# A third Strassen–Winograd level inside two of seven inner products, for three pairs of instances

## The chip, the cores and the metric

The kernel runs on one core of one Trainium2 chip. The metric is the device time of one execution in microseconds (us). Three runs of the kernel before the change are given, and one more execution of it was profiled.

## The reference

```python
batch, seq, hidden, n_experts, expert_hidden = 16, 512, 512, 8, 2048
probs = softmax(router_logits)                       # over the 8 experts
for e in range(n_experts):
    output += probs[:, :, e:e+1] * np.matmul(x, expert_weights[e])
```

The eight weighted products are one matrix product. Its left side has 16 x 512 = 8192 rows, one for each token, and 8 x 512 = 4096 columns: the token's x, scaled by the probability of each expert. Its right side is the stack of the experts' weights, 4096 rows and 2048 columns. The output is 8192 x 2048 in float32.

## The kernel before

**Two levels of a seven-product scheme.** The kernel multiplies in the Strassen–Winograd manner: a 2 x 2 x 2 product of blocks is made of seven block products instead of eight, and of sums and differences of blocks before and after. The outer level splits the output columns in two, the experts in two (0 to 3, 4 to 7) and the rows into 256-row blocks taken in twos, `a = 2q` and `b = 2q + 1`, for q from 0 to 15. Its seven products are called by the number r, and there are 16 instances (r, q) of each: `product(r, q)`. The instances with r = 1 ("P1") multiply the rows of block `a`, experts 0 to 3, by `right[1]`, the weights of these experts for the first half of the columns. They store float32 results in DRAM buffers called `kept`.

An instance has 256 rows, an inner dimension of 4 x 512 = 2048 and 1024 columns. It is split once more the same way: rows in two halves of 128 (`HP`), the inner dimension in two halves of eight chunks of 128 (`K8 = 8`; `t[0]` and `t[1]` on the left), columns in two halves of 512 (`NB`). So there are seven inner products, in the order `STEPS = (1, 5, 6, 2, 7, 3, 4)`. Each is one *step*: eight matmuls, 128 x 128 by 128 x 512, that accumulate into one bank of PSUM (`Product.step`, `mm`). `Left.op` and `Right.op` give the operands of a step. Inner products 1 and 5 both take the first half of the inner dimension, `t[0]`: product 1 its first 128 rows with the right block `w[1]`, product 5 its last 128 rows with `w[5]`, the difference of two right blocks.

**Banks.** A product uses three banks, `x`, `q` and `b`. `x` takes steps 1, 6, 7 and 4 one upon another, `q` steps 5 and 3, `b` a copy of `x` after step 1 and then step 2. After each step `Product.post` has ScalarE (ACT) copy a bank, or VectorE (DVE) add a bank and a tile in SBUF. All banks come from one pool of eight.

**Stages and slots.** Two instances run as a pair through one *stage* of 14 *slots*: step 1 of the first, step 1 of the second, step 5 of the first, and so on. Instances (1, 0) and (1, 1) are computed at the start in plain form. Stage 0 is the pair (1, 2) and (1, 3), stages 1 to 3 are (1, 4) and (1, 5), (1, 6) and (1, 7), (1, 8) and (1, 9). Stage 4 pairs (2, 9) with (1, 10).

**Order.** From stage 0 on, every engine's instructions keep the order in which the program records them. For DVE that order comes from a small planner: `later(cost, make)` queues a piece of DVE work, `slack()` moves a model clock by one slot (1.73) and runs queued pieces as long as DVE's model clock lies more than `LAG` behind PE's, and `need(task)` runs the queue up to a piece that the next step reads. `queue_lefts` queues the left blocks of the next stage (`make` for `t[0]` and `t[1]`, `queue_s2` and `queue_i` for the sums among them). `start_loads` and `finish_loads` fetch the next x and probability blocks two stages ahead; x is transposed by DMA on SP's queue. `hooks` are actions at a (stage, slot), for example the weight sums `sums_at`. Outputs are stored by POOL's DMA queue.

The left blocks `z`, the inner sums `d`, the half outputs `h` and the weights `w` live in pools of 8, 3, 12 and 15 tiles.

Of the kernel before, what the change touches and what calls it, by code (L numbers as in the profile page):

```python
# [31 lines left out]
def kernel(  # L32
# [7 lines left out]
    nc = tc.nc  # L40
    P = 128
# [8 lines left out]
    C = H // P  # L50
# [23 lines left out]
    def h_tile(shape, dtype):  # L74
        return hpool.tile(shape, dtype, name="h", tag="h")
# [8 lines left out]
    with tc.tile_pool(name="psum0", bufs=1, space=bass.MemoryType.PSUM) as psum0:  # L84
# [2 lines left out]
        every = psum0.tile([P, 8, NB], f32, name="every")  # L87
        for i in range(WARM):
            nc.tensor.matmul(every[:, i % 8, :], zero[:, 0:P], zero, start=True, stop=True)
    psum = ctx.enter_context(tc.tile_pool(name="psum", bufs=8, space=bass.MemoryType.PSUM))  # L90

    last = {}
    ordered = [False]
# [12 lines left out]
    def tt(o, a, b, op):  # L106
        dve(nc.vector.tensor_tensor(out=o, in0=a, in1=b, op=op))  # L107
# [14 lines left out]

    def bank():
        return psum.tile([P, NB], f32, name="ps", tag="ps")

    def mm(ps, z, w, start, stop):
        note(nc.tensor.matmul(ps, z, w, start=start, stop=stop, skip_group_check=True))  # L127
# [3 lines left out]
    def new_w():  # L131
        return wpool.tile([P, K8, NB], f16, name="w", tag="w")
# [31 lines left out]
    def inner_sums(b, t7=None):  # L164

        w = {1: b[0, 0], 2: b[1, 0], 3: b[1, 1], 7: t7 or b[0, 1]}

        def step(p, x, y):
            if p not in w:
                w[p] = new_w()  # L170
            tt(w[p], x, y, SUB)
        return w, {5: lambda: step(5, b[0, 1], b[0, 0]), 6: lambda: step(6, b[1, 1], w[5]),
                   4: lambda: step(4, b[1, 0], w[6]), 7: lambda: step(7, b[1, 1], b[0, 1])}

    def softmax(lg, J, pf):
        mx = h_tile([P, J], f32)
# [85 lines left out]

    def early_xp1(j, d):
        t, rows = j // 2 - 2, ds(j % 2 * P, P)
        ps = bank()
        for c in range(C):
            mm(ps[:, ds(c * P, P)], xs0[:, j, ds(c * P, P)], ident, c == 0, c == C - 1)
        evacuate(xp1[t][0][:, :, rows], ps.rearrange("p (c t) -> p c t", c=C), 0)
        ps = bank()
        mm(ps, ones, d.rearrange("p e t -> p (e t)"), True, True)  # L270
        evacuate(xp1[t][1][:, :, rows], ps.rearrange("p (e t) -> p e t", e=HE), 1)

# [33 lines left out]
    load_logits()  # L306
    early_z0(1, ds_[1])
    for n in range(2):
        ps = [bank() for _ in range(4)]
        for e in range(HE):  # L310
            if n == 0 and e < 2:
                early_z0(e + 2, ds_[e + 2])
                if e == 0:
                    ds_.append(diag_e(3))
            if n == 0 and e == 2:
                ph0.append(early_p(1))
                ds_ = [diag_j(j) for j in range(4, 8)]
                softmax_of_all()
                w, sums = inner_sums(b11, new_w())
            for c in range(C):  # L320
                for j in range(4):
                    mm(ps[j], z0[j][:, e, c], b11[e // 2, n][:, e % 2 * C + c, :],
                       e + c == 0, e == HE - 1 and c == C - 1)
            if n == 1:
                for j in ((4, 5), (6, 7), (), ())[e]:
                    early_xp1(j, ds_[j - 4])
                if e == 1:
                    sums[5]()
        for j in range(4):
            o = half()  # L330
            act(nc.scalar.copy(o, ps[j]))
            sp(kept[j // 2][n].rearrange("(p j) m -> j p m", j=2)[j % 2], o)
# [9 lines left out]
    class Task:  # L342


        def __init__(self, cost, make):
            self.cost, self.make, self.done = cost, make, False
# [17 lines left out]
        (queue.appendleft if first else queue.append)(t)  # L364
        return t

    def slack():
        clock["dve"] = max(clock["dve"], clock["pe"])
        clock["pe"] += SLOT
        while queue and clock["dve"] < clock["pe"] - LAG:  # L370
            queue.popleft().run()

    def evacuated():
        clock["dve"] = max(clock["dve"], clock["pe"]) + 0.69


    x_dram = {}
# [48 lines left out]
    class Left:  # L426
# [36 lines left out]
        def op(self, p):  # L463
# [4 lines left out]
                    3: (self.i, 0), 7: (self.i, 1)}[p]  # L468
            return t[:, :, ds(i * HP, HP)]

    class Right:


# [16 lines left out]
    class Product:  # L490
# [7 lines left out]
        def step(self, p):  # L498
            b = "q" if p in (5, 3) else "b" if p == 2 else "x"
            if p in (1, 5):  # L500
                self.banks[b] = bank()
            z, w = self.left.op(p), self.right.op(p)
            for k in range(K8):
                mm(self.banks[b], z[:, k, :], w[:, k, :], p in (1, 5) and k == 0, k == K8 - 1)
# [27 lines left out]
        def post_on_base(self, p, x, q, b):  # L532
# [13 lines left out]
            else:  # L546
                tt(o[tn], q if p in (5, 3) else x, base, ADD)


    def out_rows(q, odd, cols, tn):  # L550
        t, n = tn
# [63 lines left out]
    def product(r, q, **how):  # L615
        left, loads = left_of(r, q)
        lefts[r, q] = left
        p = None
        if r == 1:
            def sink(tn, o):  # L620
                pool(kept_rows(q)(tn), o)
            p = Product(right[1], left, sink)
        elif r == 2:
            if q >= 9:
                base = products[1, q].o.__getitem__
            else:
                base = bases[2, q] = Base(kept_rows(q))
            p = Product(right[2], left, to_out(q, 0, 0), base)
        elif r == 5:
            bases[6, q] = m1 = Base(kept_rows(q))  # L630
            m1.task = {}

            p = Product(right[5], left, to_out(q, 1, 0))
        elif r == 6:
            m1 = bases[6, q]

            def base(tn):
                need(m1.task[tn])
                return m1.t[tn]
            p = Product(right[6], left, to_out(q, 0, 1), base)  # L640
        elif r == 7:
            base = bases[7, q] = Base(lambda tn: out_rows(q, 0, 1, tn))
            p = Product(right[7], left, to_out(q, 1, 1), base)
        elif r == 4:
            p = Product(right[4], left, to_out(q, 1, 0, accum_op=ADD), products[7, q].o.__getitem__)
        else:
            p = Product(right[3], left, to_out(q, 0, 1, accum_op=ADD), **how)
        p.loads = loads
        products[r, q] = p
        return p  # L650
# [23 lines left out]
    def queue_left(left):  # L674
        if not left.task:
            left.queue_make(0)
            left.queue_s2()
            left.queue_make(1)

    def queue_lefts(stage):  # L680
        if stage < len(stages):
            for p in stages[stage]:
                queue_left(p.left)

    def run(stage):
        some = stages[stage]
        for p in some:
            p.left.queue_i()
        n = 0
        for i in range(len(some[0].steps)):  # L690
            for p in some:
                for make in hooks.get((stage, n), ()):
                    make()
                p.step(p.steps[i])
                slack()
                p.post(p.steps[i])
                n += 1
                if n == 1:
                    queue_lefts(stage + 1)
                if n == late.get(stage, 1):  # L700
                    start_loads(stage + 2)
                if n == 5:
                    store_loads(stage + 1)
                if n == 7:
                    finish_loads(stage + 2)
# [3 lines left out]
            at(stage, slot, lambda tn=tn: base.fetch(tn))  # L709


    for q in (2, 4, 6, 8):
        add(product(1, q), product(1, q + 1))
    for q in range(9, 15):
        add(product(2, q), product(1, q + 1))
    forget(*range(0, 18, 2))
    rest = [15] + list(range(9))
    for i in range(0, 10, 2):
        k = add(product(2, rest[i]), product(2, rest[i + 1]))
        for slot, tn in zip((8, 10, 12, 13), INNER):  # L720
            for q in rest[i:i + 2]:
                if q < 9:
                    fetch_at(k if tn == (1, 0) else k - 1, 3 if tn == (1, 0) else slot, bases[2, q], tn)
    xs.clear()
    k5 = add(product(5, 0), product(5, 1))
# [64 lines left out]
    def wedge_at(stage, slot, kn, e, then):  # L790
        made = []

        def begin():
            casts, made_ = wedge(kn, e)
            casts()
            made.extend(made_)

        def go_on():
            for make in made:
                later(1.22, make)  # L800
        at(stage, slot, begin)
        at(*then, go_on)
# [9 lines left out]
    def sums_at(stage, slot, r, of, ps):  # L812
        def go():
            if right[r].w is None:
                right[r].sums = right[r].build(of)
            for p in ps:
                right[r].queue_sum(right[r].sums, p)
        at(stage, slot, go)
    sums_at(3, 3, 2, b21, (5,))
    sums_at(3, 5, 2, b21, (6,))  # L820
    sums_at(3, 7, 2, b21, (7,))
    sums_at(3, 12, 2, b21, (4,))
    for i, (kn, e) in enumerate((kn, e) for kn in ((0, 0), (1, 0), (1, 1)) for e in range(2)):
        wedge_at(4 + i, 2, kn, e, (4 + i, 11))

    def fetch_at_w(stage, slot, of, what, kn):
        at(stage, slot, lambda: of.__setitem__(kn, fetch_w(what, kn)))
# [174 lines left out]
            post(p)  # L1002
    finish.step, finish.post = step_at_end, post_at_end

    need_first = [right[1].task[p] for p in (6, 7, 4)]
    for p in (2, 3):
        lefts[1, p].queue_make(0)
# [39 lines left out]
```

## Time and profile before

| | |
|---|---|
| median of 3 runs | 1376.0 us (1375.86 to 1377.01) |
| profiled execution | 1376.63 us, span 1374.9 us |
| instructions | 17480, of them 6390 matmuls and as many weight loads |
| DMA | 338.02 MB, mean 246 GB/s |

The profile is of one execution. PE is TensorE's matmuls, PEld its weight loads, which overlap them; SP and the names with a q are queues of DMA issues. In the lists of groups a row gives the line, engine and operation, output<-input with shapes and count, then busy time and the mean length of one in ns, then the idle time of the engine just before and what ended it. In the timeline a row gives start and length in us, engine, line, operation and count, and in brackets the idle time before it and its releaser. A matmul's row lasts until its result is out, longer than the time after which the next one starts. Helpers record most operations, so nearly all matmuls have line 127 and nearly all two-input DVE operations line 107.

### The profile page before, as it was taken

Reading aid. Unit: us, or ns where it says so; the run is one execution under the profiler, and the core shown is the slowest. Engines: PE = TensorE matmul, PEld = TensorE weight load, DVE = VectorE, ACT = ScalarE, POOL = GpSimd, SP = SyncE. Lnnn points to the kernel's source line nnn. Section 1 sums busy time; section 2 is a strip of 40 time slices with the busy share of each in tenths; the row PEclk is TensorE's granted clock in tenths of the full one; section 3 lists DMA queues with packets and bytes.
Section 4 is the critical chain, followed back from the end, with each engine's and each line's share of the span. In section 5 each row is a group of like instructions: output and inputs, shape, how many; then the busy total and the mean of one; then the engine's idle time right before and its main releaser. Section 6 shows DMA issues by size and latency. Waiting matters only on the chain.

```text
span 1374.9 us, 17480 instructions
## 1 busy us (share of the span) xinstructions
PE 1367.3 (99%) x6390; PEld 622.0 (45%) x6390; DVE 1108.6 (81%) x1290; ACT 183.1 (13%) x317; POOL 411.8 (30%) x652
## 2 busy tenths in 40 slices
PE   8999999999999999999999999999999999999998
PEld 4444444444444444444444444444444444444444
DVE  5846757669889888798897988889889898988882
ACT  3222111100011111111111100000000000222221
POOL 3222333241223342334232122242333322232221
PEclk9999999999999999999999999999999999999999
DMA  9998999999898998899898998988898979987786
GB/s 183 222 261 205 211 248 265 241 299 378 240 323 249 285 300 246 259 261 265 245 276 263 338 392 219 224 236 212 229 237 223 247 204 316 249 187 177 166 150 106
DMA packets 191271, 338.02 MB, mean 246 GB/s; under 512 B 52944, under 2 KB 86992, under 8 KB 187472
## 3 DMA queue, kind: packets, MB, share of 16 engines
q0 software_dynamic: 88688, 185.12, 55.8%
q1 hardware_dynamic: 98464, 123.34, 30.8%
q10 hardware_dynamic: 4032, 28.44, 5.3%
q8 instruction: 50, 0.82, 0.2%
q14 instruction: 37, 0.30, 0.1%
HBM read 207.65 MB, written 156.43 MB: 265 GB/s over the span
## 4 chain that ended last, share of the span: by engine, by line
PE 98%; DMA 2%; POOL 0%; issue 0%; ACT 0%; POOLq 0%
PE ps L127 98%; DMA w<-wd 1%; DMA w<-in_expert_weights_dram 1%; POOL w L121 0%; ACT h L999 0%; POOL ident L211 0%; POOLq L211 0%; POOLq L1031 0%
## 5 line engine op out<-in xcount | busy, mean ns | idle before, releaser
L127 PE MATMUL ps<-w,z 128*128 128x512 f16 x5416 | 1177.3, 379 | 1.3 <-DMA w<-in_expert_weights_dram 1.1
L127 PEld LDWEIGHTS <-z 128*128 128x128 f16 x5416 | 529.7, 98 | 638.6 <-DMA w<-in_expert_weights_dram 1.3
L121 POOL DMA_DIRECT2D out_dram<-h x380 | 248.9, 672 | 746.4 <-ACT h L540 373.7
L107 DVE TENSOR_TENSOR h<-ps,h 128x512 f32<-128x512 f32 x415 | 282.5, 687 | 207.6 <-PE ps L127 192.8
L107 DVE TENSOR_TENSOR z<-xT,pT 128x2048 f16<-128x2048 f16 x220 | 266.8, 1216 | 11.5 <-DMA xT<-xs 6.3
L127 PE MATMUL ps<-w,d 128*128 128x512 f16 x880 | 199.1, 379 | 0.0
L127 PEld LDWEIGHTS <-d 128*128 128x128 f16 x880 | 86.1, 98 | 103.8
L107 DVE TENSOR_TENSOR z<-z,d 128x2048 f16<-128x2048 f16 x110 | 132.1, 1215 | 0.0
L107 DVE TENSOR_TENSOR w<-w 128x1024 f16<-128x1024 f16 (+2 forms) x92 | 100.8, 1102 | 5.1 <-DMA wd<-w 3.4
L527 ACT COPY h<-ps 128x512 f32<-128x512 f32 x90 | 52.8, 586 | 373.4 <-PE ps L127 336.3
L540 ACT COPY h<-ps 128x512 f32<-128x512 f32 x64 | 37.5, 587 | 486.3 <-PE ps L127 459.9
L107 DVE TENSOR_TENSOR d<-z 128x1024 f16<-128x1024 f16 x110 | 75.2, 685 | 6.8 <-PE ps L127 5.0
L107 DVE TENSOR_TENSOR z<-z,u 128x2048 f16<-128x2048 f16 x64 | 78.4, 1225 | 2.2
L107 DVE TENSOR_TENSOR u<-xT,pT 128x2048 f16<-128x2048 f16 x64 | 77.9, 1217 | 0.0
L523 ACT COPY h<-ps 128x512 f32<-128x512 f32 x90 | 52.8, 587 | 173.9 <-PE ps L127 162.5
L121 POOL DMA_DIRECT2D w<-in_expert_weights_dram x65 | 49.0, 785 | 33.8 <-DMA wd<-w 24.0
L121 POOL DMA_DIRECT2D wd<-w x86 | 48.3, 585 | 36.0 <-DVE w L107 26.4
L107 DVE TENSOR_TENSOR ps<-ps,h 128x512 f32<-128x512 f32 (+1 forms) x66 | 45.3, 688 | 13.0 <-PE ps L127 13.0
L121 POOL DMA_DIRECT2D kept<-h x56 | 30.8, 551 | 76.8 <-ACT h L527 48.2
L107 DVE TENSOR_TENSOR h<-h 128x512 f32<-128x512 f32 (+2 forms) x69 | 45.1, 674 | 0.1
L519 ACT COPY ps<-ps 128x512 f32<-128x512 f32 x45 | 25.6, 570 | 114.6 <-PE ps L127 114.6
L107 DVE TENSOR_TENSOR z<-z 128x2048 f16<-128x2048 f16 x32 | 39.2, 1225 | 1.1
(47 smaller groups left out, 97.0 us busy)
## 6 DMA issues: line engine op xcount, KB each, us to landing
out_dram<-h POOLq DMA_DIRECT2D x380, 256.0 KB, 6.2
pT<-p_dram SPq DMA_DIRECT2D x140, 256.0 KB, 6.0
w<-wd ACTq DMA_DIRECT2D x27, 1024.0 KB, 9.9
h<-kept SPq DMA_DIRECT2D x100, 256.0 KB, 5.6
xT<-x SPq DMA_DIRECT2D x87, 256.0 KB, 5.5
wd<-w POOLq DMA_DIRECT2D x72, 256.0 KB, 5.5
w<-in_expert_weights_dram POOLq DMA_DIRECT2D x35, 512.0 KB, 10.1
h<-out_dram SPq DMA_DIRECT2D x68, 256.0 KB, 5.6
```

The costliest lines, as they stand in the source:

```text
L107: dve(nc.vector.tensor_tensor(out=o, in0=a, in1=b, op=op))
L121: note(nc.gpsimd.dma_start(out=o, in_=i, **how))
L127: note(nc.tensor.matmul(ps, z, w, start=start, stop=stop, skip_group_check=True))
L519: act(nc.scalar.copy(self.banks["b"], x))
L523: act(nc.scalar.copy(o[tn], q if p == 5 else x))
L527: act(nc.scalar.copy(o[TN[p]], b if p == 2 else x))
L540: act(nc.scalar.copy(o[tn], b))
```

## The change

In stages 1 to 3, inner products 1 and 5 of the two instances of a pair are no longer four steps of eight 512-wide matmuls. For each of the two, the left blocks of both instances are stacked, and the product is split once more into 2 x 2 x 2: the two instances as row halves, the four-chunk halves of the inner dimension (`C = 4`), and column halves of 256. Seven small products take the place of eight, for p = 1 and p = 5: 14 small products of four matmuls, 128 x 128 by 128 x 256.

The left sums for that (four operations on 128 x 1024 elements, for p = 1 and 5 at once) are made by `Thirds.make` on DVE, the right sums by `third_sums`, four operations for `w[1]` and four for `w[5]`, once, before stage 0. `by_thirds` records the 14 products. Their intermediate results go through banks `x` (one for p = 1, one for p = 5), `q` (shared by both), and `g` and `h`, which afterwards serve as the ordinary banks `x` (p = 1) and `q` (p = 5) of the first and the second instance. Between the small products ACT makes half-wide copies and DVE four half-wide additions. From slot 4 on, the stage runs as before.

The bank pool has six banks, and a pool of its own has two (`bank2`); the two hold the `q` of ordinary products and the `x` of the small ones. The names `QK` and `ND` stand for the constants 9 and 4 and change nothing else. The sum `w[5]` is made one part earlier in the plain computation at the start.

```diff
-    psum = ctx.enter_context(tc.tile_pool(name="psum", bufs=8, space=bass.MemoryType.PSUM))
+    psum = ctx.enter_context(tc.tile_pool(name="psum", bufs=6, space=bass.MemoryType.PSUM))
...
+    def bank2():
+        return psum.tile([P, NB], f32, name="pt", tag="pt", bufs=2)
...
+    def third_sums(w):
+        t = new_w().rearrange("p (s c) (h n) -> p s c h n", s=2, h=2)
+        t = {5: t[:, 0, :, 0], 6: t[:, 0, :, 1], 7: t[:, 1, :, 0], 4: t[:, 1, :, 1]}
+        b = w.rearrange("p (k c) (h n) -> p k c h n", k=2, h=2)
+        tt(t[5], b[:, 0, :, 1], b[:, 0, :, 0], SUB)
+        tt(t[6], b[:, 1, :, 1], t[5], SUB)
+        tt(t[7], b[:, 1, :, 1], b[:, 0, :, 1], SUB)
+        tt(t[4], b[:, 1, :, 0], t[6], SUB)
+        return {**t, 1: b[:, 0, :, 0], 2: b[:, 1, :, 0], 3: b[:, 1, :, 1]}
...
-        ps = bank()
+        ps = (bank, bank2)[j % 2]()
...
-        ps = [bank() for _ in range(4)]
+        ps = [bank2() if n == 0 and j < 2 else bank() for j in range(4)]
...
+                third = {1: third_sums(w[1])}
...
-                if e == 1:
+                if e == 0:
                     sums[5]()
+                elif e == 1:
+                    third[5] = third_sums(w[5])
...
-    def slack():
+    def slack(slot=SLOT, lag=LAG):
...
+    class Thirds:
+        def make(self):
+            e0, e1 = ds(0, C), ds(C, C)
+            a, b = self.a.t[0], self.b.t[0]
+            for p, x, y, op in ((5, b[:, e0], b[:, e1], ADD), (6, None, a[:, e0], SUB),
+                                (3, a[:, e1], None, SUB), (7, a[:, e0], b[:, e0], SUB)):
+                o = self.s[p] = h_tile([P, C, HQ], f16)
+                x = self.s[5] if x is None else x
+                y = self.s[6] if y is None else y
+                tt(o, x, y, op)
+        def queue(self):
+            self.a.queue_make(0)
+            self.b.queue_make(0)
+            self.task = later(2.76, self.make)
+            for left in (self.a, self.b):
+                left.queue_s2()
+            for left in (self.a, self.b):
+                left.queue_make(1)
...
-                self.banks[b] = bank()
+                self.banks[b] = (bank if p == 1 else bank2)()
...
+    def by_thirds(stage):
...
+        for n, (p, r) in enumerate(((1, 1), (5, 1), (1, 5), (1, 6), (5, 6), (5, 5), (1, 2),
+                                    (1, 7), (5, 7), (1, 3), (1, 4), (5, 2), (5, 3), (5, 4))):
+            if n in (0, 4, 7, 11):
+                for make in hooks.get((stage, slot), ()):
+                    make()
+                slot += 1
+                if slot == 2:
+                    queue_lefts(stage + 1)
+                    start_loads(stage + 2)
...
+            o = q if r in (5, 3) else g[:, cols[0]] if r == 2 else x
+            z, w = left.op(r, p // 5), third[p][r]
+            for c in range(C):
+                mm(o, z[:, c, :], w[:, c, :], (r == 1 or (p, r) == (1, 5)) and c == 0, c == C - 1)
+            slack(0.4375, LAG if n < 6 else 1.3)
+            if r == 1:
+                act(nc.scalar.copy(g[:, cols[0]], x))
+            elif r == 5:
+                act(nc.scalar.copy(keep[p][:, cols[1]], q))
+            elif r == 6:
+                act(nc.scalar.copy(keep[p][:, cols[0]], x))
+            elif r == 7:
+                evacuated(0.42)
+                tt(at_once(("h", p))[:, cols[1]], x, keep[p][:, cols[1]], ADD)
+            elif r == 3:
+                evacuated(0.42)
+                tt(g[:, cols[1]], q, keep[p][:, cols[0]], ADD)
+                if p == 1:
+                    some[0].post(1)
+            elif r == 4:
+                act(nc.scalar.copy(place["h", p][:, cols[0]], x))
+                if p == 1:
+                    some[1].post(1)
+        for product in some:
+            product.post(5)
+        return 4
...
-        n = 0
-        for i in range(len(some[0].steps)):
+        n = by_thirds(stage) if stage in thirds else 0
+        for i in range(n // 2, len(some[0].steps)):
...
+    for stage in range(1, ND):
+        thirds[stage] = Thirds(*(p.left for p in stages[stage]))
```

More of the change, by code (lines that the diff above doesn't have):

```diff
@@ L268, in early_xp1 @@
         evacuate(xp1[t][0][:, :, rows], ps.rearrange("p (c t) -> p c t", c=C), 0)
-        ps = bank()
+        ps = (bank, bank2)[j % 2]()
         mm(ps, ones, d.rearrange("p e t -> p (e t)"), True, True)
@@ L365, in later, with evacuated @@
         return t
-    def slack():
+    def slack(slot=SLOT, lag=LAG):
         clock["dve"] = max(clock["dve"], clock["pe"])
-        clock["pe"] += SLOT
-        while queue and clock["dve"] < clock["pe"] - LAG:
+        clock["pe"] += slot
+        while queue and clock["dve"] < clock["pe"] - lag:
             queue.popleft().run()
-    def evacuated():
-        clock["dve"] = max(clock["dve"], clock["pe"]) + 0.69
+    def evacuated(cost=0.69):
+        clock["dve"] = max(clock["dve"], clock["pe"]) + cost
     x_dram = {}
@@ L469, in op, with __init__ @@
             return t[:, :, ds(i * HP, HP)]
+    class Thirds:
+        def __init__(self, a, b):
+            self.a, self.b, self.s, self.task = a, b, {}, None
+        def make(self):
[15 more added lines that the diff above has]
+                left.queue_make(1)
+        def op(self, p, part):
+            need(self.task)
+            a, b = self.a.t[0], self.b.t[0]
+            z = {1: a[:, 0:C], 2: a[:, C:K8], 4: b[:, C:K8]}.get(p)
+            return (self.s[p] if z is None else z)[:, :, ds(part * HP, HP)]
     class Right:
@@ L547, in post_on_base @@
                 tt(o[tn], q if p in (5, 3) else x, base, ADD)
+    QK = 9
+    ND = QK // 2
     def out_rows(q, odd, cols, tn):
@@ L623, in product @@
         elif r == 2:
-            if q >= 9:
+            if q >= QK:
                 base = products[1, q].o.__getitem__
@@ L678, in queue_left, with at_once @@
             left.queue_make(1)
+    thirds = {}
+    def by_thirds(stage):
+        some = stages[stage]
+        left = thirds[stage]
+        cols = [ds(i * HQ, HQ) for i in range(2)]
+        place, keep = {}, {}
+        def at_once(what):
+            if what not in place:
+                t = place[what] = (bank2 if what[0] == "x" else bank)()
+                if what[0] in "gh":
+                    some["gh".index(what[0])].banks["x" if what[1] == 1 else "q"] = t
+            return place[what]
+        slot = 0
+        for n, (p, r) in enumerate(((1, 1), (5, 1), (1, 5), (1, 6), (5, 6), (5, 5), (1, 2),
[7 more added lines that the diff above has]
+                    start_loads(stage + 2)
+            x = at_once(("x", p))[:, cols[0]]
+            q = at_once("q")[:, cols[p // 5]] if n > 1 else None
+            g = at_once(("g", p))
+            if r == 1:
+                keep[p] = half()
+            o = q if r in (5, 3) else g[:, cols[0]] if r == 2 else x
[3 more added lines that the diff above has]
+            slack(0.4375, LAG if n < 6 else 1.3)
+            if r == 1:
+                act(nc.scalar.copy(g[:, cols[0]], x))
[18 more added lines that the diff above has]
+        return 4
@@ L680, in queue_lefts @@
     def queue_lefts(stage):
-        if stage < len(stages):
+        if stage in thirds:
+            if thirds[stage].task is None:
+                thirds[stage].queue()
+        elif stage < len(stages):
             for p in stages[stage]:
@@ L709, in fetch_at @@
             at(stage, slot, lambda tn=tn: base.fetch(tn))
-    for q in (2, 4, 6, 8):
+    for q in range(2, QK, 2):
         add(product(1, q), product(1, q + 1))
-    for q in range(9, 15):
+    for q in range(QK, 15):
         add(product(2, q), product(1, q + 1))
-    forget(*range(0, 18, 2))
-    rest = [15] + list(range(9))
-    for i in range(0, 10, 2):
+    forget(*range(0, 2 * QK, 2))
+    rest = [15] + list(range(QK))
+    for i in range(0, QK + 1, 2):
         k = add(product(2, rest[i]), product(2, rest[i + 1]))
@@ L721 @@
             for q in rest[i:i + 2]:
-                if q < 9:
+                if q < QK:
                     fetch_at(k if tn == (1, 0) else k - 1, 3 if tn == (1, 0) else slot, bases[2, q], tn)
@@ L818, in sums_at @@
         at(stage, slot, go)
[L819 to L822, printed above, removed]
+    sums_at(ND - 1, 3, 2, b21, (5,))
+    sums_at(ND - 1, 5, 2, b21, (6,))
+    sums_at(ND - 1, 7, 2, b21, (7,))
+    sums_at(ND - 1, 12, 2, b21, (4,))
     for i, (kn, e) in enumerate((kn, e) for kn in ((0, 0), (1, 0), (1, 1)) for e in range(2)):
-        wedge_at(4 + i, 2, kn, e, (4 + i, 11))
+        wedge_at(ND + i, 2, kn, e, (ND + i, 11))
     def fetch_at_w(stage, slot, of, what, kn):
```

## The prediction

> **What bounds the kernel now.** I read the page first: the busy times, the clock and the chain that ended last.
>
> ```profile
> span 1374.9 us, 17480 instructions
> ...
> PE 1367.3 (99%) x6390; PEld 622.0 (45%) x6390; DVE 1108.6 (81%) x1290; ACT 183.1 (13%) x317; POOL 411.8 (30%) x652
> ...
> PEclk9999999999999999999999999999999999999999
> ...
> PE 98%; DMA 2%; POOL 0%; issue 0%; ACT 0%; POOLq 0%
> ```
>
> PE is busy 1367.3 of 1374.9 us, at full clock in every slice, and the chain is PE. A busy share alone does not prove a bound, since matmuls overlap, so the list of PE's waits came next, then the three stages that the change rewrites, 65.27 to 137.78 us.
>
> ```profile
> PE every L89 <- DVE h L86: 1.3, 1, 1.3
> PE ps L127 <- DMA w<-in_expert_weights_dram: 1.1, 1, 1.1
> PE ps L127 <- DMA w<-in_x_dram: 1.0, 2, 0.6
> PE ps L127 <- DVE lg L281: 0.3, 1, 0.3
> ```
>
> ```profile
> 65.27:89.44 24.17, 24.17 (x114) 10.97 (x113) 12.53 (x15) 5.83 (x10) 7.32 (x12) 1.00 1.17 253
> 89.44:113.61 24.17, 24.17 (x114) 10.93 (x113) 11.40 (x13) 5.83 (x10) 6.79 (x12) 1.00 1.04 261
> 113.61:137.78 24.17, 24.17 (x114) 10.97 (x113) 17.55 (x15) 5.83 (x10) 6.47 (x11) 1.00 0.78 185
> ```
>
> The columns are window, length, then busy time and count of PE, PEld, DVE, ACT, POOL, and the clock. All listed waits of PE (3.7 us) lie before stage 0; in stages 1 to 3 it never waits. A stage is 14 steps of 8 matmuls, so one 512-wide matmul takes 24.17 / 112 = 0.2158 us and a step 1.726 us. Here every matmul removed shortens the kernel by its own 0.2158 us, if nothing new makes PE wait. So the questions are two: what do the new matmuls cost, and does anybody make PE wait?
>
> **PE's own work.** Per changed stage the diff takes out four steps (products 1 and 5 of both instances): 32 matmuls, 32 x 0.2158 = 6.906 us. In come 14 small products of 4 matmuls with 256 columns, 56 matmuls. The order of the changed program bears this out: 72 more matmuls in all, 3 x (56 - 32), and otherwise PE's order as it was. The price of a 256-wide matmul is at the very end of the kernel, where one step is already cut in two halves of eight:
>
> ```profile
> 1367.63 0.69 DVE L107 TENSOR_TENSOR h<-ps,h 128x512 f32<-128x512 f32 x1 [1.03 <-PE ps L127]
> 1368.50 0.42 DVE L996 COPY h<-ps 128x256 f32<-128x256 f32 x1 [0.18 <-PE ps L127]
> ```
>
> ```profile
> L127 PE MATMUL ps<-w,z 128*128 128x512 f16 x5400 | 1175.6, 379 | 1.3 <-DMA w<-in_expert_weights_dram 1.1
> L127 PE MATMUL ps<-w,z 128*128 128x256 f16 x16 | 2.1, 272 | 0.0
> ```
>
> DVE starts when the step before ends (1367.63) and again when the eight half-wide ones end (1368.50): 0.87 us for eight, 0.109 each, a little over half of 0.2158. So 56 x 0.109 = 6.10 us; saved 6.906 - 6.10 = 0.80 us a stage, **2.4 us in three stages**. Halving 0.2158 exactly would give 2.6; the upper end is that.
>
> A small product lasts 4 x 0.109 = 0.436 us; its last matmul starts 0.327 after the first and lasts 0.272 (the row's mean), so its result is there 0.60 us after its start, longer than the next product needs. That makes the waits of the next part worth walking through.
>
> **New waits of PE in the 14 products** (times from the start of the stage). The small products accumulate in turn into few banks, and a bank is read by ACT or DVE between two of them.
>
> ```profile
> 65.41 0.59 ACT L527 COPY h<-ps 128x512 f32<-128x512 f32 x1 [1.14 <-PE ps L127]
> 67.19 0.57 ACT L519 COPY ps<-ps 128x512 f32<-128x512 f32 x1 [1.19 <-PE ps L127]
> ...
> 1371.17 0.37 ACT L999 COPY h<-ps 128x256 f32<-128x256 f32 x1 [11.54 <-PE ps L127]
> ```
>
> ```profile
> L107 DVE TENSOR_TENSOR ps<-ps,h 128x256 f32<-128x256 f32 x2 | 0.8, 428 | 3.3 <-PE ps L127 3.3
> ```
>
> The first row is the copy of the last step of stage 0, the second that of stage 1's first step, which ended some 0.19 us before it (379 - 216 ns of tail, and about 0.03 for the signal): stage 1 starts at 67.00 - 1.73 = 65.27.
> - ACT ends that old copy at 0.73. Three half-wide copies follow, 0.37 each: done at 1.13, 1.50, 1.87. The products that need them, the fourth, fifth and sixth, start at 1.31, 1.74, 2.18. Margins 0.18, 0.24, 0.31.
> - The eighth product (the first "7") ends at 7 x 0.436 + 0.60 = 3.65; DVE adds it in 0.43, done 4.11. The eleventh overwrites that bank at 4.36: 0.25. DVE's third addition (after the tenth product, 4.52) ends 4.98, the thirteenth needs it at 5.23: 0.25.
> - ACT's 0.57 us copy of the first instance's bank then runs 5.01 to 5.58; the next ordinary step starts at 6.10. The second instance's copy needs a seventh bank, of six in the pool, and takes the one freed when DVE's fourth addition ends (about 6.29): 6.32 to 6.89, needed at 7.83.
>
> PE runs in order, so a late copy holds back every matmul behind it. But all margins are positive, so I take zero stall; the bounds are 0 and, if the narrow operations cost as much as the wide ones (below), 0.85 us a stage.
>
> **DVE must be free at 3.65.** Its queue is in order, so whatever stands ahead of the four additions delays PE. Added per pair are the four sums of the left side (128x1024, once each) and the four additions.
>
> ```profile
> L107 DVE TENSOR_TENSOR z<-xT,pT 128x2048 f16<-128x2048 f16 x220 | 266.8, 1216 | 11.5 <-DMA xT<-xs 6.3 <-PE ps L127 4.9 <-issue 0.3
> L107 DVE TENSOR_TENSOR d<-z 128x1024 f16<-128x1024 f16 x110 | 75.2, 685 | 6.8 <-PE ps L127 5.0
> ```
>
> ```profile
> 64.38 2.35 DVE L107 TENSOR_TENSOR z<-z,d 128x2048 f16<-128x2048 f16 x2
> ...
> 75.03 1.22 DVE L107 TENSOR_TENSOR z<-xT,pT 128x2048 f16<-128x2048 f16 x1 [5.30 <-DMA xT<-xs]
> ...
> 81.02 0.69 DVE L107 TENSOR_TENSOR h<-ps,h 128x512 f32<-128x512 f32 x1 [2.84 <-PE ps L127]
> ```
>
> That is 4 x 0.685 + 4 x 0.43 = 4.5 us, on top of 12.5 and 11.4 in stages of 23.4: room. Stage 3 makes no sums for a next stage, 17.55 + 1.7 = 19.3: room too.
> - Stage 1: before, DVE has done all that stands ahead at 66.73, with idle time in between. In the new order the second of the two last operations (about 1.2) moves behind the additions and 2.74 of sums come in: at most 66.73 - 1.2 + 2.74 = 68.3, needed 65.27 + 3.65 = 68.9. Margin 0.6 at least.
> - The second left block waits for its transpose until 75.03. Behind it now stand 1.22 + 2.74 + 1.37 + 1.22 before the addition of step 7: done at 82.3, where the row shows 81.02 for its start before. PE comes back to that bank at 65.27 + 6.10 + 8 x 1.726 = 85.2. Margin 2.9.
> - Stages 2 and 3: the new order puts the next stage's blocks behind the four additions, so DVE reaches them with several us to spare. In stage 3 the four weight sums (2.29 each, row below) are interleaved with the additions (0.69) of steps 7 and 3. Walked in that order from the stage's start: small additions to 6.3, left blocks (4 x 1.22 + 2 x 0.685) to 12.6, first sum 14.9, addition 15.6, sum 17.9, two additions 19.3, sum 21.6, addition 22.3, last sum 24.6. That is 1.2 us into stage 4, whose thirteenth step needs it; the addition that ends at 18.6 is needed at 6.10 + 9 x 1.726 = 21.6.
>
> **The start.** Eight sums on the weights, 8 x 0.685 = 5.5 us of DVE, and one old sum moved forward.
>
> ```profile
> 29.34 1.29 DVE L241 CAST xT<-ps 128x512 f16<-128x512 f32 x2 [3.73 <-PE ps L127]
> 33.67 1.29 DVE L241 CAST xT<-ps 128x512 f16<-128x512 f32 x2 [3.04 <-PE ps L127]
> 34.99 2.29 DVE L107 TENSOR_TENSOR w<-w 128x4096 f16<-128x4096 f16 x1
> 37.20 2.35 DVE L107 TENSOR_TENSOR z<-xT,pT 128x2048 f16<-128x2048 f16 x2
> ```
>
> Four sums (2.74) go into the 3.73 of idle time, the moved sum (2.29) into the 3.04, four take its place: +0.45 on the row at 37.20, so the first left block is there at about 38.9. Stage 0 starts 24.17 before 65.27, at 41.10: nothing lost. DMA issues on POOL's and SP's queues keep their order. Outside stages 1 to 3 the pools of six and two cost nothing: two ordinary products hold four banks of the six, and the two of their step 5 are free by step 3, five steps before the next stage's. The sums on the weights hold two more tiles of a pool of 15 until the last small product of stage 3; the first load that needs one of them stands in the third slot of stage 4.
>
> **Sum.** The profiled execution took 1376.63 us (span 1374.9): 1376.63 - 2.4 = 1374.2. Its median of three lies 0.6 lower, so the time asked for is 1376.0 - 2.4 = **1373.6 us**, 0.17% less. A measurement of this kernel can tell about 0.2% (2.75 us) from no change; the forecast lies just inside that.
>
> **The rivals.**
> *The banks bind.* If a half-wide copy costs what the wide one does (0.57 on ACT, 0.69 on DVE), the ACT copies end at 1.30, 1.87, and about 2.47, PE loses 0.16 and then 0.13, and DVE's first and third additions, one behind the other, end some 0.55 too late: 0.85 us a stage, 2.5 in all, and the time stays at 1376. The rows of 0.37 and 0.43 speak against it; for it, that no row shows a half-wide copy from bank to bank, and the first margin is only 0.18. A tenth.
> *Given back at a transfer.* Far behind the change PE does wait once:
>
> ```profile
> 801.07 4.86 PEld L127 LDWEIGHTS <-z 128*128 128x128 f16 x24 [0.63 <-DMA w<-wd]
> ```
>
> ```profile
> 800.00:802.00 2.00, 1.86 (x10) 0.66 (x9) 0.77 (x2) 0.00 (x0) 0.90 (x3) 1.00 1.06 436
> ```
>
> A weight fetch lands a little late. If its time were fixed by the load on the DMA engines alone, PE would reach it 2.4 us earlier and wait 2.4 us longer: 1376 again. Against it: the fetch is issued by ACT behind copies that follow PE, so it moves forward too. Under a tenth.
> *Slower: the weight load shows.* Each half-wide matmul still needs its own load.
>
> ```profile
> L127 PEld LDWEIGHTS <-z 128*128 128x128 f16 x5416 | 529.7, 98 | 638.6 <-DMA w<-in_expert_weights_dram 1.3 <-DMA w<-wd 0.6
> ```
>
> ```profile
> 6.75 1.51 PE L127 MATMUL ps<-h,w 128*128 128x128 f16 x24 [0.65 <-DMA w<-in_x_dram]
> ```
>
> If 98 ns of load no longer hid behind 109 ns of streaming, a pair would take 0.207 us, 168 of them 34.8 against 96 x 0.2158 = 20.7: +14 us, 1390. It decides from 20.7 / 168 = 0.123 us a matmul on. The second row speaks against it: 24 pairs a quarter as wide pass in 1.51 us, 0.063 each, less than one load lasts, so loads do overlap there. But the longest run of narrow matmuls in this trace is 24, and the new ones are 56. One in twenty.
> The Trainium skill, "TensorE: Matmul & The Clock Gate", Part 3 (The mechanism), says that a weight load overlaps running matmuls only when it goes to other rows of the array; these loads use all rows, and by it this rival would hold. The trace disagrees in the row of 24.
>
> **How the numbers follow.** Forecast 0.77, banks 0.10, transfer 0.08, weight load or another way to slower 0.05. The three runs of before spread over 1.15 us, so 2.4 us saved can be measured as over 2.75: I give a fifth of the forecast's chance to that, 0.15. Faster 0.15, same 0.80, slower 0.05. The range: below, 0.6 us of spread, 1373.0; above, the two middle rivals in part, 1375.3.
>
> **What would show it.** Right: steps 1 and 5 of stages 1 to 3 replaced by blocks of 6.10 us, stages of 23.4 us (slot-1 copies 23.4 apart), no PE wait in them, DVE some 4.5 us busier in stages 1 and 2. Wrong: PE waits for ACT at the fourth to sixth product or for DVE at the eleventh and thirteenth; half-wide matmuls over 0.115 us apart; a longer wait near 800 us.

## The result and the profile after

| | before | after |
|---|---|---|
| median of 19 runs | 1376.47 us (1375.86 to 1377.07) | 1373.69 us (1372.79 to 1375.49) |
| span of the profiled execution | 1374.9 us | 1372.3 us |

The ratio is 0.9982, with a 95% interval of 0.9976 to 0.9988: the change saves 0.18% by the ratio, 2.8 us by the medians and 1.7 to 3.3 us by the interval. Forecast were 1373.6 us and 2.4 us saved. The ratio lies within 0.2% of no change, and the interval still excludes no change at all.

The page of the changed kernel, in the lines that were shown of before:

```profile
span 1372.3 us, 17676 instructions
...
PE 1365.2 (99%) x6462; PEld 629.2 (46%) x6462; DVE 1125.6 (82%) x1322; ACT 190.2 (14%) x341; POOL 411.3 (30%) x652
...
PEclk9999999999999999999999999999999999999999
```

72 matmuls more, yet PE is busy 2.1 us less, still at 99% and full clock. The list of PE's waits, and stages 1 to 3 by windows (length, then busy time and count of PE, PEld, DVE, ACT, POOL, the clock, DMA share and GB/s):

```profile
PE every L89 <- DVE h L86: 1.3, 1, 1.3
PE pt L130 <- DMA w<-in_expert_weights_dram: 1.1, 1, 1.1
PE ps L130 <- DMA w<-in_x_dram: 0.6, 1, 0.6
PE ps L130 <- DVE lg L295: 0.3, 1, 0.3
```

```profile
65.33:88.71 23.38, 23.38 (x138) 13.33 (x137) 18.67 (x24) 8.20 (x18) 7.31 (x12) 1.00 1.18 254
88.71:112.09 23.38, 23.38 (x138) 13.29 (x137) 15.11 (x20) 8.23 (x18) 6.72 (x12) 1.00 1.09 262
112.09:135.47 23.38, 23.38 (x138) 13.33 (x137) 18.16 (x18) 8.23 (x18) 6.51 (x11) 1.00 0.81 195
```

No new wait stands in the list, and each of the three stages lasts 23.38 us where it lasted 24.17, PE busy from end to end. That is 0.79 us a stage and 2.38 us in three. DVE's load rises by 6.1, 3.7 and 0.6 us in the three windows.

The two spans differ by 2.6. Two things outside the stages make up the rest. Stage 0 starts 0.1 us later, by ACT's copy of its first step, first before, then after:

```profile
43.02 0.57 ACT L519 COPY ps<-ps 128x512 f32<-128x512 f32 x1 [0.38 <-PE ps L127]
```

```profile
43.13 0.57 ACT L567 COPY ps<-ps 128x512 f32<-128x512 f32 x1 [0.38 <-PE ps L130]
```

And the wait for a weight fetch near 800 us is absent here: PE is busy through that window. In the profile of before it cost 0.3 us, 0.14 of idle time in the window that the prediction shows and 0.16 that the tail of the last matmul covers.

```profile
799.00:801.00 2.00, 2.00 (x11) 0.92 (x10) 0.51 (x2) 0.00 (x0) 0.54 (x1) 1.00 1.00 410
```

```profile
798.42 3.64 PEld L130 LDWEIGHTS <-z 128*128 128x128 f16 x18 [0.25 <-DMA w<-wd]
```

The second row is the first weight load that needs the fetched weights. It still waits for them, 0.25 us where it was 0.63 before, but no longer so long that PE stands still. It starts at 798.42 where it was 801.07, 2.65 us earlier, so the fetch moved forward with PE.

So 2.6 = 2.38 - 0.1 + 0.3. Both extras end with the arrival of a DMA transfer: PE's last wait before stage 0, for the experts' weights, ends at 10.88 us here and at 10.75 before. The start moves between executions: in the runs of one stage and of doubled copies below, which up to there have the same instructions, stage 1 starts at 65.10 and 64.81, here at 65.33. What moves the late fetch is left open by the runs below.

The margins of the walk can be read in stage 1, which starts at 65.33. ACT's rows, then DVE's:

```profile
65.57 0.59 ACT L575 COPY h<-ps 128x512 f32<-128x512 f32 x1 [1.14 <-PE ps L130]
66.05 0.70 ACT L767 COPY ps<-pt 128x256 f32<-128x256 f32 x2
66.88 0.37 ACT L769 COPY h<-ps 128x256 f32<-128x256 f32 x1
...
70.42 0.57 ACT L567 COPY ps<-ps 128x512 f32<-128x512 f32 x1 [1.90 <-DVE ps L107]
```

```profile
66.62 1.22 DVE L107 TENSOR_TENSOR z<-z,d 128x2048 f16<-128x2048 f16 x1
69.09 0.87 DVE L107 TENSOR_TENSOR ps<-pt,h 128x256 f32<-128x256 f32 x2 [1.25 <-PE pt L130]
69.89 0.43 DVE L107 TENSOR_TENSOR ps<-ps,h 128x256 f32<-128x256 f32 x1
71.20 0.43 DVE L107 TENSOR_TENSOR ps<-ps,h 128x256 f32<-128x256 f32 x1 [0.88 <-PE ps L130]
```

From the stage's start, the second of the narrow copies ends at 66.75 - 65.33 = 1.42 (walk: 1.50), the third at 1.92 (1.87). DVE's second addition ends at 4.63 (4.54), the third at 4.99 (4.98), the fourth at 6.30 (6.29). DVE stood idle for 1.25 us before the first addition, where the prediction granted 0.6 at least.

### The profile page after: what moved, and what is told of

The parts are those of the page before. It is cut to its first block, busy times and chain, and to the rows that moved or that the text cites. A ratio compares the mean times of both kernels' runs of the same rounds, so it can differ in the third digit from the quotient of the medians.

```text
span 1372.3 us, 17676 instructions
## 1 busy us (share of the span) xinstructions
PE 1365.2 (99%) x6462; PEld 629.2 (46%) x6462; DVE 1125.6 (82%) x1322; ACT 190.2 (14%) x341; POOL 411.3 (30%) x652
## 4 chain that ended last, share of the span: by engine, by line
PE 99%; DMA 1%; POOL 0%; issue 0%; ACT 0%; POOLq 0%
PE ps L130 71%; PE pt L130 28%; DMA w<-in_expert_weights_dram 1%; POOL w L121 0%; ACT h L1110 0%; POOL ident L225 0%; POOLq L225 0%; POOLq L1144 0%
## 5 line engine op out<-in xcount | busy, mean ns | idle before, releaser
L130 PE MATMUL ps<-w,z 128*128 128x512 f16 (+1 forms) x3648 | 804.7, 378 | 0.0
L130 PE MATMUL pt<-w,z 128*128 128x512 f16 (+1 forms) x1744 | 392.7, 376 | 1.1 <-DMA w<-in_expert_weights_dram 1.1
L107 DVE TENSOR_TENSOR h<-ps,h 128x512 f32<-128x512 f32 x246 | 168.4, 688 | 128.9 <-PE ps L130 122.4
L107 DVE TENSOR_TENSOR h<-pt,h 128x512 f32<-128x512 f32 x169 | 115.6, 688 | 67.1 <-PE pt L130 62.5
L107 DVE TENSOR_TENSOR w<-w 128x1024 f16<-128x1024 f16 (+2 forms) x100 | 106.1, 1070 | 4.6 <-DMA wd<-w 2.9
L588 ACT COPY h<-ps 128x512 f32<-128x512 f32 x64 | 37.5, 586 | 486.0 <-PE ps L130 457.5
L575 ACT COPY h<-ps 128x512 f32<-128x512 f32 x90 | 52.7, 586 | 373.5 <-PE ps L130 334.5
```

The costliest lines, as they stand in the source:

```text
L575: act(nc.scalar.copy(o[TN[p]], b if p == 2 else x))
L588: act(nc.scalar.copy(o[tn], b))
```

## The experiments

Seven kernels. Each time stands beside that of the kernel before in runs on the same chip: 1376.25 us for the pools alone, one stage, four stages and the doubled copies, 1376.05 for the other three.

**The pools alone.** The changed kernel without small products and third-level sums:

```diff
-    for stage in range(1, ND):
+    for stage in range(1, 1):
         thirds[stage] = Thirds(*(p.left for p in stages[stage]))
```

(and without the two calls of `third_sums`, the sum `w[5]` in its old place).

> The two bank pools (six and two) alone; inner products 1 and 5 stay ordinary steps in all stages, and no third-level sums are made. Theory A (the time follows PE's own work alone: stages of 24.17 us as before): no change, 1376.5 us. Rival P (a part of the 2.8 us measured for the whole change, about the 0.4 that the 2.38 of three stages leaves over, comes from the pools): about 1376.1. Under A a wait near 800 us may or may not show in the profile, and costs at most 0.3.

Measured: 1376.05 us, ratio 0.9997 (0.9988 to 1.0006). No effect of the pools is seen; the interval is more than 1 us wide on either side, so it does not exclude the 0.4 us of rival P. In its list of PE's waits, the late fetch is back, longer than in the profile of before:

```profile
PE ps L130 <- DMA w<-wd: 0.6, 1, 0.6
```

With the covered 0.16 it cost 0.8 us here, 0.3 before the change and nothing after it, in kernels whose order there is the same. One execution of each kernel was profiled. PE waits at this place in the two profiles without small products, before and here. It does not wait there in the four profiles with small products and QK at 9 (the changed kernel, one stage, doubled copies, one pool), nor in the run of half-wide matmuls everywhere. Whether the wait comes and goes with the execution or the small products make it rarer is not shown.

**One stage.**

```diff
-    for stage in range(1, ND):
+    for stage in range(1, 2):
```

> The whole change, but small products in stage 1 alone (stages 2 and 3 in ordinary steps). Theory A: a third of 2.38, that is 0.79 us less than before, 1375.7; stage 1 lasts 23.38 us, stages 2 and 3 last 24.17. Rival P (a fixed part from pools or the start): 0.79 + 0.4, about 1375.3.

Measured: 1375.82 us, ratio 0.9999 (0.9990 to 1.0008); the runs alone cannot tell 0.79 us from nothing. The profile can. The windows of stages 1, 2 and 3:

```profile
65.10:88.48 23.38, 23.38 (x138) 13.32 (x137) 16.27 (x20) 8.47 (x18) 7.33 (x12) 1.00 1.20 267
88.48:112.65 24.17, 24.17 (x113) 10.96 (x112) 11.38 (x13) 5.83 (x10) 6.73 (x12) 1.00 1.11 212
112.65:136.82 24.17, 24.17 (x113) 10.95 (x112) 17.55 (x15) 5.83 (x10) 6.54 (x11) 1.00 0.87 241
```

The gain sits in the stage with small products, and the stages behind it do not give it back.

**Four stages.**

```diff
-    QK = 9
+    QK = 11
```

> The constant QK at 11 instead of 9: five pairs of P1 instances in place of four, and small products in stages 1 to 4. Theory A: 4 x 0.79 = 3.17 us less than before, about 1373.3 by that alone, or 0.79 less than the changed kernel, 1372.9. Rival T (a transfer or DVE's queue gives it back: two more instances go through DRAM, and stage 5 takes the weight sums that stage 4 had): no less than the changed kernel, 1373.7 or more.

Measured: 1380.43 us, ratio 1.0030 (1.0018 to 1.0041). Slower than before, against theory A. The windows of its stages 1 to 4, and one window far behind them:

```profile
64.68:88.06 23.38, 23.38 (x138) 13.32 (x137) 18.53 (x24) 8.20 (x18) 7.33 (x12) 1.00 1.22 251
88.06:111.44 23.38, 23.38 (x138) 13.30 (x137) 15.11 (x20) 8.23 (x18) 7.44 (x13) 1.00 1.13 245
111.44:134.82 23.38, 23.38 (x138) 13.32 (x137) 15.11 (x20) 8.24 (x18) 6.53 (x11) 1.00 0.96 258
134.82:158.20 23.38, 23.38 (x138) 13.30 (x137) 18.16 (x18) 8.23 (x18) 5.07 (x9) 1.00 0.51 142
340.00:350.00 10.00, 5.32 (x19) 2.09 (x18) 6.25 (x8) 1.17 (x2) 1.08 (x2) 0.83 1.01 366
```

All four stages have their 23.38 us. In the last window PE is busy only 5.32 of 10 us. PE's wait there, and what DVE waited for (the addition at 346.48 is the one that ends PE's wait):

```profile
347.22 5.01 PE L130 MATMUL ps<-w,z 128*128 128x512 f16 x16 [4.68 <-DVE h L107]
```

```profile
341.42 0.69 DVE L107 TENSOR_TENSOR h<-pt,h 128x512 f32<-128x512 f32 x1 [4.27 <-DMA h<-kept]
...
344.38 0.69 DVE L107 TENSOR_TENSOR h<-pt,h 128x512 f32<-128x512 f32 x1 [1.14 <-DMA h<-kept]
...
346.48 0.69 DVE L107 TENSOR_TENSOR h<-ps,h 128x512 f32<-128x512 f32 x1 [0.81 <-DMA h<-kept]
```

DVE, in order, waits for half outputs that come back from DRAM (`kept`), and PE waits for DVE. With QK at 11 two more instances take that way. Is the loss theirs, or do the small products share in it?

**Five pairs, no small products.** QK at 11 and the pools, no third level (the edit of the first run on top of `QK = 11`).

> Five pairs of P1 instances (QK at 11) and the two pools, but no small products in any stage. Theory A1 (the 7.7 us of waits behind stage 3 in the run with four stages come from the fifth pair itself: two more instances go through DRAM, and their loads land late between weight fetches; the small products gain their 3.17 in full): 3.17 more than that run, about 1383.6. Theory A2 (the transfers of that place are due at fixed times, so what PE gains before them it waits out there): the same as that run, 1380.4. Rival A3 (the small products themselves, with DVE's added work, make the late waits): about 1376.3, as before the change.

Measured: 1384.23 us, ratio 1.0057 (1.0044 to 1.0070). The same wait stands in the list of its PE waits:

```profile
PE ps L130 <- DVE h L107: 4.1, 1, 4.1
```

QK at 11 alone costs 8 us. Which of the things that it moves makes the transfers late (two more instances through DRAM, the weight sums one stage later) was not tried. The small products on top take 3.8 us off by the medians, measured on two chips, and 1381.7 - 1378.7 = 3.0 by the spans of the two profiled executions, where four stages are worth 4 x 0.79 = 3.17. The five runs here spread over 4.5 us, so how much of the 3.17 is kept cannot be told to a few tenths. But no run with the small products took as long as the fastest without them (1381.27 and 1381.39): A2 and A3 are out, and A1 holds in the main. A transfer that comes late at a place 200 us on does not swallow what PE gained.

**Copies and additions twice.** Takes the margins away.

```diff
             if r == 1:
-                act(nc.scalar.copy(g[:, cols[0]], x))
+                for _ in range(2):
+                    act(nc.scalar.copy(g[:, cols[0]], x))
```

(and the same for the copies of r = 5 and 6 and the additions of r = 7 and 3).

> The changed kernel with each of the six half-wide copies that free a bank, and each of the four half-wide additions, issued twice in a row (same values). It takes away the margins of the walk: ACT's second copies end at 1.42, 2.08 and 2.74 us from the stage's start, PE would lose 0.16, 0.23 and 0.22 at the fourth, fifth and sixth product, 0.23 at the tenth and 0.58 at the thirteenth. Theory W (PE waits exactly as that walk has it): 1.45 us a stage, 4.3 in all, 1378.0. Rival S (there is more room than the walk says, for instance because only the first copy is waited for): 1373.7. Theory W with the margins counted too small: between the two.

Measured: 1378.75 us, ratio 1.0020 (1.0011 to 1.0029), slower than before. Its stage 1 by window, and PE's starts in it:

```profile
64.81:89.98 25.17, 24.29 (x138) 13.26 (x136) 20.16 (x28) 9.97 (x24) 7.32 (x12) 1.00 1.18 244
```

```profile
64.81 1.04 PE L130 MATMUL pt<-w,z 128*128 128x256 f16 x8
65.68 0.60 PE L130 MATMUL ps<-w,h 128*128 128x256 f16 x4
66.36 1.26 PE L130 MATMUL pt<-w,h 128*128 128x256 f16 x8
67.71 0.60 PE L130 MATMUL ps<-w,h 128*128 128x256 f16 x4
...
68.58 1.08 PE L130 MATMUL pt<-w,h 128*128 128x256 f16 x8
69.75 0.60 PE L130 MATMUL ps<-w,h 128*128 128x256 f16 x4
70.25 0.60 PE L130 MATMUL pt<-w,z 128*128 128x256 f16 x4
70.68 0.60 PE L130 MATMUL ps<-w,z 128*128 128x256 f16 x4
71.84 0.60 PE L130 MATMUL ps<-w,h 128*128 128x256 f16 x4 [0.56 <-DVE ps L107]
```

A row of 8 matmuls is two products. Starts should lie 0.436 apart. From the third product to the fourth it is 0.68, so 0.24 lost (walk: 0.16). From the fourth to the sixth 1.35 instead of 0.87, 0.48 lost (0.45). From the eighth to the tenth 0.30 (0.23), to the eleventh 0.06 (none), from the twelfth to the thirteenth 1.16, 0.72 lost (0.58). The sum is 1.80 us a stage against the walk's 1.45: theory W, with 0.03 to 0.14 more at each of these places than it counted. PE's waits fall on the products that the walk names and, but for the 0.06, on no others.

**Half-wide matmuls everywhere.** From the kernel before:

```diff
             for k in range(K8):
-                mm(self.banks[b], z[:, k, :], w[:, k, :], p in (1, 5) and k == 0, k == K8 - 1)
+                for c in (ds(0, HQ), ds(HQ, HQ)):
+                    mm(self.banks[b][:, c], z[:, k, :], w[:, k, c],
+                       p in (1, 5) and k == 0 and c.start == 0, k == K8 - 1)
```

> The kernel before, with every 512-wide matmul of every ordinary step cut into two of 256 columns with the same weights (the weights are loaded twice; same result): 6152 of them, so 6152 more. Theory A (0.1092 us each, weight load hidden, also in long runs): 12304 x 0.1092 - 6152 x 0.2158 = 16 us more, about 1392. Rival L (a weight load of 98 ns shows behind a half-wide matmul): 0.207 x 12304 - 1328 = over 1200 us more, about 2590.

Measured: 1391.15 us, ratio 1.0109 (1.0095 to 1.0123). Its busy times from the page, and 100 us of its middle:

```profile
PE 1383.5 (100%) x12542; PEld 1224.5 (88%) x12542; DVE 1110.3 (80%) x1290; ACT 182.8 (13%) x317; POOL 411.4 (30%) x652
```

```profile
100.00:200.00 100.00, 100.00 (x918) 89.64 (x917) 66.19 (x69) 17.66 (x31) 29.64 (x50) 1.00 0.89 219
```

918 matmuls in 100 us are 0.109 us each, through thousands of them, with PEld at 88 to 90%. With the 0.1092 us that the stages of 23.38 us give, (23.38 - 80 x 0.2158) / 56, cutting a matmul in two costs 2 x 0.1092 - 0.2158 = 0.0026 us more, 16 us over 6152; measured are 15.1. The load stays hidden, with little left over: rival L is out.

**One pool of eight banks.**

```diff
-    psum = ctx.enter_context(tc.tile_pool(name="psum", bufs=6, space=bass.MemoryType.PSUM))
+    psum = ctx.enter_context(tc.tile_pool(name="psum", bufs=8, space=bass.MemoryType.PSUM))
...
     def bank2():
-        return psum.tile([P, NB], f32, name="pt", tag="pt", bufs=2)
+        return bank()
```

> The changed kernel with one pool of eight banks for all, instead of six and two. Theory A: in the order of this kernel no bank comes later than it is needed, so the time is that of the changed kernel, 1373.7, with stages of 23.38. Rival P (the pool of its own is needed: PE waits for a bank that ACT or DVE still reads): some tenths of a us in each of three stages, 1374.5 or more.

Measured: 1373.82 us, ratio 0.9983 (0.9974 to 0.9992), as the changed kernel. One of its stages:

```profile
64.59:87.97 23.38, 23.38 (x137) 13.32 (x136) 18.48 (x24) 8.33 (x18) 7.33 (x12) 1.00 1.20 259
```

For time the second pool is not needed. The output is another one, however, off by a relative error of 0.13; the last section has a likely reason. The instructions and their sizes are the same, so the time can be read as it stands.

## Why the prediction was right

- **PE bounds stages 1 to 3.** Right: they are PE work from end to end before and after, and the stage shortened by exactly what PE's work did.
- **The price of a half-wide matmul, 0.109 us, read from two rows at the kernel's end.** Right: 24.17 - 23.38 = 0.79 us a stage for the 0.80 of the sum, and 918 in 100 us when they run without a break. Halving a full-wide matmul would have promised 0.86.
- **No new wait.** Right, by the windows. The doubled copies show that the margins were no more than the walk said: six more copies and four more additions of 0.4 us turn the gain into a loss. The rival "the banks bind" described a real mechanism; the narrow copies just are short enough.
- **DVE's cover.** Right with room to spare. The step that was most cautious was the transpose: the prediction let it land at 75.03 as before and had the addition of step 7 done at 82.3. In stage 1 after the change:

```profile
74.74 1.23 DVE L107 TENSOR_TENSOR z<-xT,pT 128x2048 f16<-128x2048 f16 x1 [0.85 <-issue]
...
81.01 0.69 DVE L107 TENSOR_TENSOR h<-ps,h 128x512 f32<-128x512 f32 x1
```

  It ran at 81.01 to 81.70, as early as before. "DVE some 4.5 us busier in stages 1 and 2" came out as 6.1 and 3.7, since left-block operations of 1.2 us, or parts of one, fell on the other side of a stage's border.
- **Given back at a transfer.** It did not happen, and for the reason that the prediction gave: the weight load behind the fetch started 2.65 us earlier, as PE got there earlier. With four stages, too, the gain remains beside its own control. But the wait at this fetch cost between 0 and 0.8 us in the profiles, and the prediction took it as fixed.
- **The size.** The medians moved by 2.8 us, the stages by 2.38. The other 0.4 lies inside the interval (1.7 to 3.3). The profiles show a start and a late fetch that differ by tenths; whether the change shifts them on average is open. That the time itself, 1373.69, falls within 0.1 us of the forecast is luck in part: the kernel before measured 1376.47 in these runs, 0.5 above the median that the forecast started from, and the saving came out 0.4 larger; the two nearly cancel.

## What to carry to other kernels

Where one engine is busy without a break, count its instructions at their own measured spacing, not at half of the next larger size: here the whole effect was 32 x 0.2158 against 56 x 0.1092. Then walk the handovers between engines one by one from the rows, since a margin of two tenths of a us in a chain of copies is all that stands between such a gain and a loss. A change that gains a fixed amount per stage need not pay more when a constant is widened to give it more stages, if the same constant moves other work too, here more half outputs through DRAM: run the constant alone as a control.

## What the runs showed of the hardware

A wait of 4.7 us costs PE more than itself. In the run with four stages, the 16 matmuls behind it took 5.01 us, where 16 at 0.216 and a tail of 0.16 make 3.6. The granted clock is 0.83 over the window shown, and 0.50 in the stretch from 347.20 to 349.00 us, right behind the wait. The run of five pairs shows the same: 4.10 us without work, then 5.03 us for 16 matmuls. The Trainium skill, "TensorE: Matmul & The Clock Gate", Part 1, says that the clock falls to half after an idle window of about 3.4 us; the trace agrees, and here that added 1.4 us.

A full set of weights can be loaded behind every half-wide matmul: in the run of halves PEld is busy 88% of the span beside PE's 100%. That goes against the sentence of the Trainium skill, "TensorE: Matmul & The Clock Gate", Part 3, on loads and rows of the array that the prediction weighed.

The changed output of the one-pool run fits a rule of the Trainium skill, "PSUM — Partial Sum Buffer" (The four PSUM rules): the first matmul of a group clears a mark over the whole bank, and a later matmul that is not a first one adds where the mark is set and overwrites where it is clear. The small products' `x` banks are written by PE in one half only; in a pool of their own they are not handed to users that add onto values put there by ACT or DVE. That this is the cause was argued, not tried.
